# A hybrid decoder layer: the mixing's output product by Strassen's method, with low parts of its weight sums made by DMA

## The chip, the cores and the metric

One core of a Trainium2 chip runs the whole layer in one launch. The metric is device time in microseconds. TensorE multiplies, VectorE (DVE) and ScalarE (ACT) do elementwise work, GpSimd (POOL) does a little of it and issues DMAs of its own, SyncE (SP) issues the other DMAs.

## The reference, cut to what matters

A layer of 512 tokens, width 1024, with four sublayers, each followed by a LayerNorm of the weighted residual: a SwiGLU FFN, a token mixing, a cross-attention into 256 memory tokens, and another SwiGLU FFN. The mixing and what follows it:

```python
o = o * rsqrt(mean(o**2) + eps) * gnorm * silu(g)      # four gated heads, 512 channels
p = causal_multiscale_pool(v, pool_w, pool_scale)      # four pool groups, 512 channels
merged = concatenate([o, p], axis=-1)                  # (512, 1024)
h = layernorm(ALPHA * h + merged @ w_mix_out)          # w_mix_out (1024, 1024)
h = layernorm(ALPHA * h + memory_attention(h, mem, wq, wk, wv, wo))
```

The change concerns `merged @ w_mix_out`.

## The kernel before

**Numbers in two parts.** Every operand of a large product is held as a high and a low part in a reduced 32-bit format. `split` (L66 to L68) makes them: ScalarE casts the high part (L67), VectorE subtracts it from the source for the low one (L68). A product is then three matmuls: high by high, high by low, low by high (`mm3`, L55). `wblock` (L71) loads a weight block of 128 x 1024 by SyncE (L74) into one of 7 `raw` buffers and splits it, into two of 7 `q` buffers or, with `stay`, into one of the 13 large `b8` buffers. `one_behind` is called once for each weight block; it may send one action of a list (below) on GpSimd's queue, behind a tiny `seen` operation (L322) that waits for the block's high part.

**Order.** Each engine runs its own list of instructions in order. A planner makes these lists from the code: where an instruction's inputs or buffers aren't expected yet, a later one that is ready goes ahead. So transposes that the code puts ahead of a product stand in the trace between its matmuls.

**The two FFNs by Strassen's method.** `strassen_gemm` (L325) computes an FFN's output product from quarters of both sides with seven half-size products instead of eight, over three pairs of PSUM banks u, v and w: a11 by b11, s1 by t1, s2 by t2, a12 by b21, s4 by b22, s3 by t3, a22 by t4. The left sums are made by VectorE just ahead (`combine`, L347). The right sums t1 to t4 are sums of weight blocks: class `Sums` copies one block to a DRAM tile (`copy`, L281) and adds another by an accumulating DMA (`add`, L290), all on GpSimd's queue. The results go into h by L378 (with the residual's scale) and L381 (without).

**The mixing.** Projections by TensorE for the forget gates (`pf`), queries (`pq`), pool groups (`pv`), values (`vps`) and output gates (`pgt`), then the levels of the chunked scan, the states, and for each of four token tiles the output o: matmuls L876 and L878, squares on ScalarE, `rs` by a power on GpSimd (L886), the scaled o by VectorE (L887). The keys of the memory tokens are one `mem_key(k)` each (24 matmuls of 128 x 256): key 0 ahead of the states, 1 and 2 between the o tiles and their transposes (`ot`, L898), 3 to 7 after the output product. Each transposed tile is gated (L900) into `og` and split into `mg`; the pool groups have been split into `mg` by `pool_out`.

**Its output product.** `out_gemm` (called for "mo") goes over two halves of 512 columns. In a half it takes four weight blocks of 256 rows in the order 2, 3, 0, 1: the pool's first, then the heads'. The first blocks run block by block over four token tiles, the last ones (two in the first half, all four in the second) tile by tile, so that tile after tile is finished: L240 adds the bank to h, L243 takes statistics, `ln_tile` (L167 to L180, with a power on GpSimd, L174) normalises, `transpose_h` (L192) transposes into `moT` for the next stage. There is then `mem_key(3)` to `mem_key(7)`, and the memory's values `vm`, neither of which needs `moT`.

**The second FFN's sums.** From the queries on, two of three weight blocks send an action of the second FFN's list; what is left goes inside that FFN (`Sums.step`, L307).

Of the kernel before, what the change touches and what calls it, by code (L numbers as in the profile page):

```python
# [21 lines left out]
FF = 2816  # L22
FT = FF // P
H = 4
NMEM = 256
LEVELS = [1, 2, 4, 8, 16, 32, 64]
ALPHA = 2.0 ** 0.25
LN_EPS = 1e-5
# [6 lines left out]
def layer_kernel(ctx: ExitStack, tc: tile.TileContext, a, out):  # L35
    nc = tc.nc
# [4 lines left out]
    sm = ctx.enter_context(tc.tile_pool(name="sm", bufs=6))  # L41
    st = ctx.enter_context(tc.tile_pool(name="st", bufs=4))
# [20 lines left out]
    def raw4(shape, name):  # L63
        return wp.tile(shape, F32, tag="raw", name=name, bufs=7)

    def split(src, hi, lo, cast=nc.scalar.copy):  # L66
        cast(out=hi, in_=src)  # L67
        nc.vector.tensor_tensor(out=lo, in0=src, in1=hi.bitcast(F32), op=ALU.subtract)  # L68


    def wblock(src, name, stay=False):  # L71
        n = src.shape[-1]
        raw = raw4([P, n], f"raw_{name}")
        nc.sync.dma_start(raw, src)  # L74
        if stay:
            both = b8([P, 2, n], F32R, f"ws_{name}")
            hi, lo = both[:, 0, :], both[:, 1, :]
        else:
            hi, lo = q4([P, n], f"whi_{name}"), q4([P, n], f"wlo_{name}")
        split(raw, hi, lo)  # L80
        one_behind(hi)
        return hi, lo

# [182 lines left out]
    class Sums:  # L266
# [16 lines left out]
        def add(self, behind):  # L283

            if self.adds and self.adds[0] in self.T:
                p, b = self.adds.pop(0)
                x = {"t1": lambda: of_block(self.w, 1, self.kb1[b]), "t3": lambda: of_block(self.w, 1, self.kb2[b]),
                     "t2": lambda: self.T["t1", b], "t4": lambda: self.T["t2", b]}[p]()
                with tc.issue_after(behind):
                    nc.gpsimd.dma_start(self.T[p, b], x, accum_op=ALU.add, max_dma_last_dim=8192)  # L290
# [34 lines left out]
    def strassen_gemm(groups, S_, alpha, g, b, eps, name, final=False, pre=None, ys=None):  # L325
# [61 lines left out]
        if len(groups) == 1:  # L387
            quarter_["s1"] = [raw4([P, 4, 256], f"{name}s1")]
        else:
            s1 = b8([P, 2, 4, 256], F32, f"{name}s1")  # L390
            s1_ = [sm.tile([P, n, 256], F32, tag="s1", name=f"{name}s1_{n}", bufs=2) for n in (2, 1)]
            quarter_["s1"] = [s1[:, 0], s1[:, 1], *s1_]
        product(L, "b11", u, True)
        combine("s1", "a21", "a22", ALU.subtract)
        L = left("s1")
# [56 lines left out]
        if final or ys is not None:  # L452
            return None if final else tiles
        return [(tiles[k // 2][:, k % 2, 0, :], tiles[k // 2][:, k % 2, 1, :]) for k in range(KT)]


    def proj_T(w, X, n=S, name="pj"):
# [259 lines left out]
    def mslot(k):  # L717
        return mg[k // 2][:, k % 2, 0, :], mg[k // 2][:, k % 2, 1, :]

    pooled = {}  # L720

    def pool_in(g):
# [73 lines left out]
    for li, m in enumerate(LEVELS):  # L796
        tv = Tl[li].rearrange("p (n two) -> p n two", two=2)
        for g in range(2):
# [3 lines left out]
            if m < 64:  # L802
                def right(x, src=False):

                    return (x.rearrange("p (n two m) -> p n two m", two=2, m=m)[:, :, 1, :] if src
                            else x.rearrange("p (n m) -> p n m", m=m))
# [56 lines left out]
                    op0=ALU.mult, op1=ALU.add)  # L863
        states.append(Sn)

    for q in range(2):
        mg[q] = b8([P, 2, 2, S], F32R, f"mg{q}")


    os_ = []  # L870
# [22 lines left out]
    for c, o in enumerate(os_):  # L893
        cs = slice(c * P, (c + 1) * P)
        pt = tr_ps("ot")
        for hd in range(H):
            hs = slice(hd * P, (hd + 1) * P)
            nc.tensor.transpose(pt[:, hs], o[:, hs], ident)  # L898
        og = sm.tile([P, S], F32, tag="sg", name="og")
        nc.vector.scalar_tensor_tensor(  # L900
            out=og.rearrange("p (h d) -> p h d", h=H), in0=pt.rearrange("p (h d) -> p h d", h=H),
            scalar=gn[:, 0:1], in1=GS[:, :, cs], op0=ALU.mult, op1=ALU.mult)
        ov = og.rearrange("p (a b n) -> p a b n", a=2, b=2)
        for q in range(2):
# [174 lines left out]
```

## Time and profile before

| | us |
|---|---|
| median of 3 runs (lowest, highest) | 1041.16 (1040.78, 1041.31) |
| the profiled execution | 1040.28 |
| its span, first to last instruction | 1038.5 |
| TensorE busy | 1024.5 |
| VectorE busy | 830.7 |
| ScalarE busy | 508.3 |
| GpSimd busy | 137.4 |

The profile is of one execution. Its rows name line, engine, operation, output and inputs by the program's tile names, shapes and count, then busy time in us and the mean duration of one in ns, and after a second bar the idle time of the engine just ahead of them and what ended it. Matmuls overlap, so 390 ns for one is its latency; the spacing of consecutive ones is what counts. A stage row gives the window, its length, each engine's busy time with the number of instructions, the granted clock, the DMA engines' share and GB/s.

### The profile page before, as it was taken

What the parts mean: (1) busy time and instruction counts of PE and PEld (TensorE: products, weight loads), DVE (VectorE), ACT (ScalarE), POOL (GpSimd) and SP (SyncE); (2) the same over time, 40 slices, a digit from 0 to 9 for tenths busy, and PEclk for the clock granted to TensorE, in tenths of its full rate; (3) what the DMA queues carried; (4) which work ended last, traced back from release to release, by engine and by line L of the source; (5) the groups of instructions that cost most, each with busy time, mean ns of one, the idle gap of its engine ahead of it and who ended that gap; (6) DMA issues with size and microseconds to landing.
All of it is one profiled execution on the core that took longest, in us unless ns stands there. A gap on an engine that the chain in (4) does not pass through costs nothing. (4 is left out here: it accounts for less than half of the span.)

```text
span 1038.5 us, 17839 instructions
## 1 busy us (share of the span) xinstructions
PE 1024.5 (99%) x6898; PEld 926.9 (89%) x6898; DVE 830.7 (80%) x1360; ACT 508.3 (49%) x879; POOL 137.4 (13%) x212
## 2 busy tenths in 40 slices
PE   9999999999999999999999999999999999999995
PEld 8999999998887988879888988889999999988884
DVE  7999888889989645886686356589988888889885
ACT  5566555566644422235324345236555555565731
POOL 0011111215200101002212100110000000025000
PEclk9999999999999999999999999999999999999998
DMA  9375776578966455544819741603333332359761
GB/s 359 130 243 164 220 230 201 144 232 263 285 212 241 145 155 150 148 128 131 239 60 339 207 110 61 203 23 123 90 104 124 100 102 86 119 178 241 240 236 68
DMA packets 46148, 177.36 MB, mean 171 GB/s; under 512 B 6512, under 2 KB 7792, under 8 KB 42736
## 3 DMA queue, kind: packets, MB, share of 16 engines
q1 hardware_dynamic: 40176, 130.09, 36.3%
q0 software_dynamic: 5888, 46.14, 18.0%
q8 instruction: 54, 0.88, 0.3%
q14 instruction: 30, 0.25, 0.1%
HBM read 174.11 MB, written 48.23 MB: 214 GB/s over the span
## 5 line engine op out<-in xcount | busy, mean ns | idle before, releaser
L547 PE MATMUL f2u<-xt,qf2s 128*128 128x256 f32 x480 | 60.7, 283 | 0.0
L547 PE MATMUL f1u<-xt,qf1s 128*128 128x256 f32 x480 | 60.7, 283 | 0.0
L547 PEld LDWEIGHTS f1u<-xt,qf1s 128*128 128x128 f32 x480 | 59.0, 192 | 0.0
L547 PEld LDWEIGHTS f2u<-xt,qf2s 128*128 128x128 f32 x480 | 59.0, 192 | 0.0
L174 POOL TENSOR_TENSOR rstd<-ve,mhalf 128x1 f32<-128x1 f32 x16 | 15.6, 973 | 153.9 <-DVE ve L172 153.9
L68 DVE TENSOR_TENSOR wlo_wv<-raw_wv,whi_wv 128x1024 fp32r<-128x1024 f32 x12 | 14.7, 1224 | 23.4 <-PE pq L57 8.5
L547 PE MATMUL f2w<-xoT,qf2a 128*128 128x256 f32 x240 | 32.1, 284 | 0.0
L547 PE MATMUL f1u<-xT,qf1a 128*128 128x256 f32 x240 | 32.1, 283 | 0.0
L547 PE MATMUL f2u<-xoT,qf2a 128*128 128x256 f32 x240 | 32.1, 283 | 0.0
L547 PE MATMUL f1w<-xT,qf1a 128*128 128x256 f32 x240 | 32.1, 284 | 0.0
L307 POOL TENSOR_TENSOR seen<-qf2a,mhalf 128x1 f32<-128x1 f32 x10 | 5.9, 593 | 188.2 <-ACT qf2a L67 188.2
L547 PE MATMUL f1u<-xt,qf1a 128*128 128x256 f32 x240 | 30.7, 284 | 0.0
L547 PE MATMUL f1v<-xt,qf1s 128*128 128x256 f32 x240 | 30.7, 284 | 0.0
L547 PE MATMUL f2v<-xt,qf2s 128*128 128x256 f32 x240 | 30.4, 284 | 0.0
L547 PE MATMUL f1v<-xT,qf1s 128*128 128x256 f32 x240 | 30.4, 283 | 0.0
L547 PE MATMUL f2v<-xoT,qf2s 128*128 128x256 f32 x240 | 30.4, 284 | 0.0
L547 PE MATMUL f2u<-xt,qf2a 128*128 128x256 f32 x240 | 30.4, 283 | 0.0
L547 PEld LDWEIGHTS f1w<-xT,qf1a 128*128 128x128 f32 x240 | 30.3, 192 | 0.1
L547 PEld LDWEIGHTS f2w<-xoT,qf2a 128*128 128x128 f32 x240 | 30.3, 192 | 0.0
L547 PEld LDWEIGHTS f1u<-xT,qf1a 128*128 128x128 f32 x240 | 30.2, 192 | 0.0
L547 PEld LDWEIGHTS f2u<-xoT,qf2a 128*128 128x128 f32 x240 | 30.2, 192 | 0.0
L547 PEld LDWEIGHTS f1u<-xt,qf1a 128*128 128x128 f32 x240 | 29.6, 192 | 0.1
(435 smaller groups left out, 3305.8 us busy)
## 6 DMA issues: line engine op xcount, KB each, us to landing
f1t<-in_w1out POOLq DMA_DIRECT2D x30, 512.0 KB, 8.0
f2t<-in_w2out POOLq DMA_DIRECT2D x30, 512.0 KB, 6.6
raw_f1t<-f1t SPq DMA_DIRECT2D x20, 512.0 KB, 4.4
raw_f2t<-f2t SPq DMA_DIRECT2D x20, 512.0 KB, 4.9
raw_f2g<-in_w2in SPq DMA_DIRECT2D x17, 512.0 KB, 3.7
raw_f2u<-in_w2in SPq DMA_DIRECT2D x17, 512.0 KB, 3.8
raw_f1u<-in_w1in SPq DMA_DIRECT2D x15, 512.0 KB, 5.9
raw_f1b<-in_w1out SPq DMA_DIRECT2D x15, 512.0 KB, 7.5
```

The lines of the kernel that those rows point to most:

```text
L68: nc.vector.tensor_tensor(out=lo, in0=src, in1=hi.bitcast(F32), op=ALU.subtract)
L174: nc.gpsimd.tensor_tensor(out=rstd, in0=ve, in1=mhalf[:, 0:1], op=ALU.pow)
L307: ins = nc.gpsimd.tensor_tensor(out=seen, in0=q[:, 0, 0:1].bitcast(F32), in1=mhalf[:, 0:1], op=ALU.mult).ins
L547: nc.tensor.matmul(o, q[:, w, wsl], x[k][r], start=opens and k == 0 and n == 0, stop=ends and k == 3 and n == 2, skip_group_check=True)
```

## The change

- The product goes to a new function, `strassen_heads`: seven half-size products of 24 matmuls, left side A1 (pool groups) and A2 (heads) held unsplit in 32 bits (`mgp`, `mgh`) and cut into token halves. `pool_out` and the gating of heads write those and split nothing.
- b22, t3 and t4 run tile by tile (`by_tiles`); after b22 tiles 0 and 1 are normalised, after t4 tiles 2 and 3.
- For the right sums t1 to t4 (eight blocks) the low part comes in another way: ScalarE writes the high part, then its negative into the low part's place, and an accumulating DMA from GpSimd adds the source block to it in SBUF.
- All transposes of h stand behind keys 3 to 7 (`fill`).
- The product's own right sums (8 copies, 8 adds) are put ahead of the second FFN's list, which now starts at the forget gates with an action per weight block; no action during this product and the attention's output product, four of five blocks in between.
- In `strassen_gemm` a branch for a single group goes, which neither FFN took.

```diff
-    def wblock(src, name, stay=False):
+    def wblock(src, name, stay=False, by_dma=False):
...
-        split(raw, hi, lo)
+        if by_dma:
+            nc.scalar.copy(out=hi, in_=raw)
+            nc.scalar.activation(lo, hi.bitcast(F32), AF.Copy, scale=-1.0)
+            nc.gpsimd.dma_start(lo, src, accum_op=ALU.add, max_dma_last_dim=8192)
+        else:
+            split(raw, hi, lo)
         one_behind(hi)
...
+    def strassen_heads(A1, A2, S_, alpha, g, b, eps, name, ys=None, fill=None, pre=None):
...
+        A = {"a11": A1[:, :, lo], "a12": A2[:, :, lo], "a21": A1[:, :, hi], "a22": A2[:, :, hi]}
+        direct = {"b11": (0, S_.kb1), "b21": (0, S_.kb2), "b22": (1, S_.kb2)}
...
+        def left(p):
+            T = b8([P, 4, 2, 256], F32R, f"{name}{p}")
+            split(A[p], T[:, :, 0, :], T[:, :, 1, :])
+            return parts(T)
...
+        def right(p):
+            for i in range(2):
+                if p in direct:
+                    yield wblock(S_.w[direct[p][0], direct[p][1][i]], f"{name}{p}{i}")
+                else:
+                    yield wblock(S_.T[p, i], f"{name}{p}{i}", True, True)
...
+        A["s1"] = raw4([P, 4, 256], f"{name}s1")
+        product(left("a11"), "b11", u, True)
+        combine("s1", "a21", "a22", ALU.subtract)
+        L = left("s1")
+        for t in range(2):
+            add(t, 0, u[t], True)
+        product(L, "t1", v, True)
+        combine("a21", "a11", "a21", ALU.subtract)
+        combine("a11", "s1", "a11", ALU.subtract)
+        L = left("a11")
+        for t in range(2):
+            add(2 + t, 1, v[t], True)
+        product(L, "t2", u)
+        L = left("a12")
+        for t in range(2):
+            add(t, 1, u[t], True, ALU.subtract)
+        product(L, "b21", w, True, True)
+        combine("a12", "a12", "a11", ALU.add)
+        L, L3 = left("a12"), left("a21")
+        for t in range(2):
+            add(t, 0, w[t], False, last=True)
+        B22, T3 = list(right("b22")), list(right("t3"))
+        L4, T4 = left("a22"), list(right("t4"))
+        GB = ln_bcast(g, b)
+        for t in by_tiles(L, B22, v, True):
+            add(t, 1, v[t], False, last=True)
+            ln_tile(t, stats[t], GB, eps)
+        for t in by_tiles(L3, T3, u):
+            add(2 + t, 1, u[t], False, ALU.subtract, last=True)
...
+        for t in by_tiles(L4, T4, u, True):
...
+            add(2 + t, 0, u[t], True, last=True)
+            ln_tile(2 + t, stats[2 + t], GB, eps)
...
+        if fill is not None:
+            fill()
+        for t in range(0 if fill is not None else 2, NT):
+            transpose_h(t, tiles, ys)
...
+    sums_mo = Sums(a["wmixo"], "mo", [2, 3], [0, 1])
+    sums2 = Sums(a["w2out"], "f2", *FFN_BLOCKS)
+    todo_behind += sums_mo.actions() + sums2.actions()
+    pace[:] = 0, 1, 1
     pf01 = proj_T2(wf, X1, "pf")
...
-    sums2 = Sums(a["w2out"], "f2", *FFN_BLOCKS)
-    todo_behind += sums2.actions()
-    pace[:] = 0, 2, 3
...
-    mg = {q: b8([P, 2, 2, S], F32R, f"mg{q}") for q in (2, 3)}
...
+    mg = [None, b8([P, 4, S], F32, "mgp")]
...
-        mh, ml = mslot(4 + g)
-        nc.scalar.activation(mh, pm, AF.Copy, scale=psc[:, g:g + 1])
-        nc.vector.scalar_tensor_tensor(out=ml, in0=pm, scalar=psc[:, g:g + 1], in1=mh.bitcast(F32),
-                                       op0=ALU.mult, op1=ALU.subtract)
+        nc.scalar.activation(mg[1][:, g, :], pm, AF.Copy, scale=psc[:, g:g + 1])
...
-        og = sm.tile([P, S], F32, tag="sg", name="og")
         nc.vector.scalar_tensor_tensor(
-            out=og.rearrange("p (h d) -> p h d", h=H), in0=pt.rearrange("p (h d) -> p h d", h=H),
+            out=mg[0][:, :, cs], in0=pt.rearrange("p (h d) -> p h d", h=H),
...
-        for q in range(2):
-            split(ov[:, q], mg[q][:, :, 0, cs], mg[q][:, :, 1, cs])
-
-    X2 = out_gemm(a["wmixo"], KT, mslot, ALPHA, a["ln2_g"], a["ln2_b"], LN_EPS, "mo", order=[2, 3, 0, 1])
...
-    for k in range(3, KT):
-        mem_key(k)
+    def more_keys():
+        pace[:] = 0, 4, 5
+        for k in range(3, KT):
+            mem_key(k)
+
+    pace[:] = 0, 0, 1
+    X2 = strassen_heads(mg[1], mg[0], sums_mo, ALPHA, a["ln2_g"], a["ln2_b"], LN_EPS, "mo", fill=more_keys)
...
     ys, wx = [], []
+    pace[:] = 0, 0, 1
     X3 = out_gemm(a["wo"], KT, lambda k: (OT[k // 2][:, k % 2, 0, :], OT[k // 2][:, k % 2, 1, :]),
```

More of the change, by code (lines that the diff above doesn't have):

```diff
@@ L386, in strassen_gemm @@
         L = left("a11")
[L387 to L392, printed above, removed]
+        s1 = b8([P, 2, 4, 256], F32, f"{name}s1")
+        s1_ = [sm.tile([P, n, 256], F32, tag="s1", name=f"{name}s1_{n}", bufs=2) for n in (2, 1)]
+        quarter_["s1"] = [s1[:, 0], s1[:, 1], *s1_]
         product(L, "b11", u, True)
@@ L454, in strassen_gemm, with combine, block, product @@
         return [(tiles[k // 2][:, k % 2, 0, :], tiles[k // 2][:, k % 2, 1, :]) for k in range(KT)]
+    def strassen_heads(A1, A2, S_, alpha, g, b, eps, name, ys=None, fill=None, pre=None):
+        stats = [st.tile([P, 2, 6], F32, tag=f"stats{t}", name=f"stats{t}", bufs=1) for t in range(NT)]
+        lo, hi = slice(0, 256), slice(256, 512)
+        A = {"a11": A1[:, :, lo], "a12": A2[:, :, lo], "a21": A1[:, :, hi], "a22": A2[:, :, hi]}
[4 more added lines that the diff above has]
+            return parts(T)
+        def combine(o, x, y, op):
+            nc.vector.tensor_tensor(out=A[o], in0=A[x], in1=A[y], op=op)
+        def right(p):
[3 more added lines that the diff above has]
+                else:
+                    assert (p, i) in S_.T and (p, i) not in S_.adds
+                    yield wblock(S_.T[p, i], f"{name}{p}{i}", True, True)
+        def block(t, i, w, L, ps, opens, ends):
+            tsl = slice(t * P, (t + 1) * P)
+            for j in range(2):
+                k, csl = 2 * i + j, slice(j * 512, (j + 1) * 512)
+                ah, al = L[k][0][:, tsl], L[k][1][:, tsl]
+                for n, (x, y) in enumerate(((ah, w[0]), (ah, w[1]), (al, w[0]))):
+                    nc.tensor.matmul(ps, x, y[:, csl], start=opens and k == 0 and n == 0, stop=ends and k == 3 and n == 2,
+                                     skip_group_check=True)
+        def product(L, p, ps, opens=False, ends=False):
+            for i, w in enumerate(right(p)):
+                for t in range(2):
+                    block(t, i, w, L, ps[t], opens, ends)
+        def by_tiles(L, ws, ps, ends=False):
+            for t in range(2):
+                for i, w in enumerate(ws):
+                    block(t, i, w, L, ps[t], False, ends)
+                yield t
+        def add(t, hf, ps, scale, op=ALU.add, last=False):
+            sl = slice(hf * 512, hf * 512 + 512)
+            if scale:
+                nc.vector.scalar_tensor_tensor(out=h[t][:, sl], in0=h[t][:, sl], scalar=float(alpha), in1=ps,
+                                               op0=ALU.mult, op1=op)
+            else:
+                nc.vector.tensor_tensor(out=h[t][:, sl], in0=h[t][:, sl], in1=ps, op=op)
+            if last:
+                nc.vector.bn_stats(stats[t][:, hf, :], h[t][:, sl])
+        u, v, w = ([mm_ps(f"{name}{n}{t}") for t in range(2)] for n in "uvw")
+        A["s1"] = raw4([P, 4, 256], f"{name}s1")
[12 more added lines that the diff above has]
+        L = left("a12")
+        for t in range(2):
+            add(t, 1, u[t], True, ALU.subtract)
+        product(L, "b21", w, True, True)
+        combine("a12", "a12", "a11", ALU.add)
+        L, L3 = left("a12"), left("a21")
+        for t in range(2):
+            add(t, 0, w[t], False, last=True)
[7 more added lines that the diff above has]
+            add(2 + t, 1, u[t], False, ALU.subtract, last=True)
+        tiles = [quarter(f"{name}T{q}") if ys is not None else b8([P, 2, 2, S], F32R, f"{name}T{q}") for q in range(4)]
+        if fill is None:
+            transpose_h(0, tiles, ys)
+        for t in by_tiles(L4, T4, u, True):
+            if fill is None and t == 0:
+                transpose_h(1, tiles, ys)
+            add(2 + t, 0, u[t], True, last=True)
+            ln_tile(2 + t, stats[2 + t], GB, eps)
+            if t == 0 and pre is not None:
+                pre()
+        if fill is not None:
+            fill()
+        for t in range(0 if fill is not None else 2, NT):
+            transpose_h(t, tiles, ys)
+        return (tiles if ys is not None else
+                [(tiles[k // 2][:, k % 2, 0, :], tiles[k // 2][:, k % 2, 1, :]) for k in range(KT)])
@@ L864, in layer_kernel @@
         states.append(Sn)
-    for q in range(2):
-        mg[q] = b8([P, 2, 2, S], F32R, f"mg{q}")
+    mg[0] = b8([P, 4, S], F32, "mgh")
     os_ = []
```

4 lines of the change are left out of this document (removed).

## Prediction

> **What bounds the kernel now.** I read the page first, then who waits for whom on TensorE, then the busy times by stage.
>
> ```profile
> span 1038.5 us, 17839 instructions
> PE 1024.5 (99%) x6898; PEld 926.9 (89%) x6898; DVE 830.7 (80%) x1360; ACT 508.3 (49%) x879; POOL 137.4 (13%) x212
> PEclk9999999999999999999999999999999999999998
> ```
> ```profile
> PE idle L103 <- DVE mhalf L157: 1.1, 1, 1.1
> PE trh L192 <- DVE h L180: 0.5, 1, 0.5
> PE po L56 <- ACT PT L67: 0.2, 1, 0.2
> PE f2u L367 <- DVE h L381: 0.2, 1, 0.2
> ```
> ```profile
> 230.00:260.00 30.00, 30.00 (x133) 24.79 (x132) 29.92 (x34) 19.20 (x24) 16.48 (x14) 1.00 0.79 254
> 260.00:300.00 40.00, 40.00 (x178) 33.08 (x177) 36.23 (x42) 22.03 (x27) 6.82 (x13) 1.00 0.90 275
> 490.00:505.00 15.00, 15.00 (x74) 12.33 (x73) 12.57 (x19) 7.46 (x14) 3.95 (x8) 1.00 0.94 252
> 505.00:523.00 18.00, 18.00 (x81) 14.67 (x80) 11.71 (x18) 3.16 (x3) 3.60 (x5) 1.00 0.67 226
> 523.00:538.00 15.00, 14.97 (x78) 11.99 (x78) 12.31 (x26) 3.15 (x9) 1.54 (x2) 1.00 0.01 4
> 538.00:554.00 16.00, 16.00 (x133) 15.65 (x132) 14.04 (x25) 8.54 (x16) 4.20 (x7) 1.00 0.69 224
> 493.30:522.90 29.60, 29.60 (x130) 24.28 (x130) 3.43 (x5) 1.00 0.81 239
> ```
>
> The page says TensorE 99% at full clock. The four waits are all that this view lists for TensorE in the whole span: 2.0 us. In the stage table the columns are length, then busy time of TensorE, weight loads, VectorE, ScalarE and GpSimd, granted clock, DMA share, GB/s. The mixing's output product (490 to 538) runs with TensorE busy throughout and VectorE at 65 to 84%. The last row counts that product's own matmuls in its densest stretch: 130 in 29.60 us, 0.2277 us each, one after the other. So the end is set by the list of TensorE's work: a matmul taken out is worth 0.2277 us, unless a new wait takes its place.
>
> The Trainium skill, page "Perfetto Trace Analysis", section Identifying the Most-Contended Engine, warns that matmul busy time overstates how close TensorE is to its limit and points to the weight loads instead. Here they are busy 24.28 of 29.60 us, 82%; by that rule a fifth of the stretch could be slack, and 24 matmuls fewer would bring about 4.5 us. I go by the even spacing and the missing waits.
>
> **What is removed.**
>
> ```profile
> L223 PE MATMUL mops<-whi_mo,mg 128*128 128x512 f32 x40 | 16.0, 399 | 0.0
> L223 PE MATMUL mops<-ws_mo,mg 128*128 128x512 f32 x24 | 9.4, 394 | 0.0
> L68 DVE TENSOR_TENSOR wlo_mo<-raw_mo,whi_mo 128x1024 fp32r<-128x1024 f32 x5 | 6.1, 1220 | 2.6 <-PE pk L58 1.5 <-issue 1.1
> L67 ACT CAST whi_mo<-raw_mo 128x1024 fp32r<-128x1024 f32 x5 | 5.2, 1047 | 0.0
> L240 DVE SCALAR_TENSOR_TENSOR h<-h,mops 128x512 f32<-128x512 f32 x8 | 5.5, 685 | 7.4 <-PE mops L225 7.3
> L243 DVE BATCH_NORM_STATS2 stats<-h 128x6 f32<-128x512 f32 x8 | 5.5, 693 | 0.2
> L177 DVE SCALAR_TENSOR_TENSOR h<-h,mv,G 128x512 f32<-128x512 f32 x8 | 5.6, 744 | 0.0
> L180 DVE SCALAR_TENSOR_TENSOR h<-h,rstd,B 128x512 f32<-128x512 f32 x8 | 5.6, 747 | 0.1
> L68 DVE TENSOR_TENSOR mg<-og,mg 128x256 fp32r<-128x256 f32 x8 | 2.9, 419 | 0.0
> L900 DVE SCALAR_TENSOR_TENSOR og<-ot,gn,GS 128x512 f32<-128x512 f32 x4 | 2.9, 745 | 0.0
> L68 DVE TENSOR_TENSOR wlo_wk<-raw_wk,whi_wk 128x1024 fp32r<-128x1024 f32 x6 | 7.3, 1212 | 0.4 <-PE pgt L57 0.3
> L68 DVE TENSOR_TENSOR KM<-pk,KM 128x256 fp32r<-128x256 f32 x6 | 2.5, 422 | 0.4 <-ACT KM L67 0.2
> ```
>
> L223, L224 and L225 issue one matmul each, so there are 3 x (40 + 24) = 192. Seven half-size products of 2 weight blocks x 2 token tiles x 2 x 3 are 168. Gone: 24 x 0.2277 = 5.46 us of TensorE's list. The transposes stay 32 and keys 3 to 7 stay 5; they only change place. One Strassen product is 24 x 0.2277 = 5.46 us, and all that feeds it must keep that pace.
>
> **What is added on VectorE.** Sums of quarters are tensor_tensor on 128x1024, as in the FFN products; adds into h without the scale too:
>
> ```profile
> L347 DVE TENSOR_TENSOR f1g<-f1g,f1g x2: 1218/1218/1219, 266.7 to 268.5; 128x1024 f32<-128x1024 f32 x2
> L381 DVE TENSOR_TENSOR h<-h,f1w x2: 670/674/679, 290.2 to 292.5; 128x512 f32<-128x512 f32 x2
> 484.10 0.39 PE L878 MATMUL o<-Sall,QP 128*128 128x128 f32 x2
> 487.78 0.69 DVE L887 TENSOR_TENSOR o<-o,rs 128x512 f32<-128x512 f32 x1 [1.12 <-POOL rs L886]
> 489.58 1.04 PE L898 MATMUL ot<-ident,o 128*128 128x128 f32 x8
> 538.50:546.20 7.70, 7.70 (x64) 7.56 (x63) 0.85 (x2) 0.74 (x2) 1.00 0.39 113
> ```
>
> The last row is of the keys' matmuls alone: 7.70/64 = 0.12 us each, 2.89 us for a key of 24.
>
> First the chain to the second product. Before, two pool blocks (48 matmuls, 10.9 us) stood ahead of anything that needs the heads; now only the a11 product (5.46 us) does. The last head tile is normalised at 488.5. Then VectorE has two key halves (0.84), four gated heads (2.98), the s1 sum (1.22), ScalarE's cast (1.05), s1's low part (1.22): 7.3 us, ready at 495.8. The eight splits L68 of heads (2.9) are gone from there. TensorE has 16 transposes (2 x 1.04) and one product from 489.58: it wants s1 at 497.1. The slack is 1.3 us, one weight split of 1.22 slipped in uses it up, two make TensorE wait 1.1 us. I take 0.4 (bounds 0 and 1.1).
>
> Then the pace. From 488.5 to the end of the fourth product (497.1 + 3 x 5.46 = 513.5) VectorE gets: heads and keys 3.82, four sums 4.88, five left low parts 6.10, four right ones 4.88 (b21, b22), six adds 4.11: 23.8 us in 25.0, 95%. With the low parts of t1 and t2 on VectorE too it would be 28.7, over the room; the DMA takes these. The first FFN's Strassen stretch, the two rows from 230 to 300, had VectorE at 29.92 of 30 and 36.23 of 40 and TensorE lost nothing. I take 0.2 for it (bounds 0 and 1).
>
> A new wait: t4's first tile goes into the bank that t3 filled, after VectorE has added that bank to h. Only t3's second tile (2.73 us) stands between, and VectorE then has the LayerNorms of tiles 0 and 1 queued. No transposes stand between as they do in the first FFN. The nearest row is f2u waiting 0.2 for L381. The upper end is a LayerNorm's last four operations ahead of that 0.67 add: 2.98 + 0.67 - 2.73 = 0.9. I take 0.3, near the row.
>
> **What is added on ScalarE, GpSimd and DMA.** Eight right blocks get a second ScalarE pass (8 x 1.05 us; ScalarE is busy 7.46 of 15.00 at most) and an accumulating DMA from GpSimd into SBUF. No such transfer into SBUF is in the trace; accumulating ones in DRAM are:
>
> ```profile
> f2t<-f2t POOLq DMA_DIRECT2D x10, 512.0 KB, 7.3
> L290 POOL DMA_DIRECT2D f2t<-f2t x12: 763/796/854, 420.9 to 956.7; - x12
> DMA to landing us min/median/max: 4.3/7.1/9.5
> ```
>
> Of the 13 large buffers 11 or 12 hold QP, scT, V, GS, Sall, the merged halves, memory, keys and a11 until the last o matmul ends at 484.5. From there, the second t1 block needs up to four ScalarE passes (4.2), the issue (0.80) and the landing (7.3): 496.8, and 499.0 with the worst landing. TensorE wants it half a product after 497.1, at 499.8. t2, t3 and t4 are wanted 5 us or more later each, with buffers free earlier than that. So I cost it at nothing; the cover is the a11 product and keys 1 and 2 ahead of it. If the landing took twice the median, as could be with DMA at 0.94, t1 would be 4.3 us late.
>
> The Trainium skill, page "DMA: Bandwidth & Descriptors", section Anatomy of one DMA (SWDGE path), fits 2.0 us plus bytes over 436e3 per us: an estimate of 3.2 us for 512 KB. The trace's 7.3 us is more than twice that. By the page t1 would land at 492.7 and the late-landing rival below would vanish; the sum stays.
>
> GpSimd's queue is in order: a transfer that waits for ScalarE's second pass holds what stands behind it, the rs and rstd powers. rs stands on the head chain, so a t1 issue placed ahead of it costs it up to 0.80 us each; it is within the 0.4 above. SyncE loads 14 blocks instead of 16 for this product.
>
> Moved: 16 actions for this product's sums go ahead of the second FFN's on GpSimd, one per weight block from the forget gates on, and the last goes out behind the second gate's block, with two gates, three keys and the o stage still ahead of the product. More of the second FFN's sums then run inside that FFN. The first FFN runs all its sums inside itself, with no TensorE wait in the list above. Nothing is charged (bounds 0 and 0.5). Keys 3 to 7, with loads and splits, stand behind t4 instead of behind the transposes; the transposes then run beside 96 matmuls of the values (21.9 us) that don't need them, so the LayerNorm tail is hidden.
>
> **Sum.** -5.46 + 0.4 + 0.2 + 0.3 = -4.56. The profiled execution took 1040.28 (span 1038.5), the median of the runs is 1041.16, 0.88 above it; I take the difference off the median: 1036.6.
>
> **Rivals.** *Low parts late.* TensorE waits for SBUF-accumulating DMAs at t1 and, less, at t2. For: 512 KB into SBUF was never timed, DMA 0.94 at 490 to 505. Against: GpSimd and ScalarE have room and the later three have time. Price 2 to 5 us above the sum: 1039 to 1041, about no change.
>
> *VectorE's tail starves the keys* (slower). The first FFN's tail shows the small steps of a LayerNorm, and what else stands there:
>
> ```profile
> 306.26 0.20 DVE L170 BATCH_NORM_AGGREGATE mv<-stats 128x2 f32<-128x12 f32 x1
> 306.37 1.18 DVE L68 TENSOR_TENSOR wlo_f1t<-raw_f1t,whi_f1t 128x1024 fp32r<-128x1024 f32 x1
> 307.45 0.15 DVE L172 TENSOR_SCALAR ve<-mv 128x1 f32<-128x1 f32 x1
> ```
>
> From the end of the fourth product VectorE has: two w tiles 2 x (0.67 + 0.69) = 2.73, a22's low part 1.22, two v tiles, two t3 tiles 2.73, two t4 tiles. A tile with LayerNorm is 0.69 + 0.69 + 2 x 0.74 + 2 x 0.75 + 0.35 = 4.71, so 25.5 in all, against three products of 16.4. When TensorE comes to key 3 VectorE is 9.1 us behind. If a key's low part (1.21) stood behind all that, TensorE would wait 10.3 us: 1041.16 - 5.46 + 0.6 + 10.3 = 1046.6. Each key split ahead of the backlog covers 2.89 us; it decides below two: with one, 1043.7, with two 1040.8. Against it are the three rows: in the first FFN's tail a weight split is placed inside a LayerNorm, between two of its dependent steps, so later weights don't stand behind it.
>
> *The saving isn't there.* If the gain follows the weight loads it is 4.5 instead of 5.46: 1037.6, inside the range.
>
> **Chances.** Forecast (with the smaller saving) 0.78; late low parts 0.14, a third of it still faster; starved keys 0.08, three quarters of it slower. 0.2% is 2.1 us, about what a measurement tells from no change. Faster (under 1039.1): 0.78 + 0.05 = 0.83. Slower: 0.06. Same: 0.11. The range: its low end is the full 5.46 and half a microsecond more from the waits that TensorE has now, 1035.2. The bounds above add 1.1 + 1 + 0.9 + 0.5 - 0.9 taken = 2.6 to the sum, 1039.2; up to 1039.6 it takes in the near part of the late landings and leaves out under 2 in 10.
>
> **What would show it.** Right: TensorE's matmul count 24 lower, busy near 1020, its wait list under 4 us, accumulating transfers into SBUF landing in 5 to 9 us. Wrong: a wait of TensorE on a DMA (the first rival), on the keys' or values' low parts by L68 (the second), on s1's left part by more than 1.1 us, or on h at t4 by more than 0.9; or TensorE without such waits and a gain under 4 us, which would say that matmuls were not worth their spacing.

## The result and the profile after

The changed kernel takes 1054.87 us (median), where the kernel before took 1041.16. Single runs far above the others of their kernel, one of 2043.85 us here, count in the medians and are left out of the ratios and intervals; without it the runs here go from 1051.94 to 1055.54, with a median of 1054.31. The ratio is 1.0124, with a 95% interval of 1.0108 to 1.0141: 12.9 us more (11.2 to 14.7), where 4.6 us less was forecast. The profiled execution took 1055.54.

First the changed kernel's page: span, busy times, TensorE's granted clock in 40 slices.

```profile
span 1053.7 us, 17870 instructions
PE 1022.8 (97%) x6874; PEld 924.4 (88%) x6874; DVE 836.9 (79%) x1363; ACT 526.5 (50%) x892; POOL 160.8 (15%) x238
PEclk9999999999999999999899999999999999999997
```

6898 - 6874 = 24 matmuls are gone, as forecast, but TensorE now waits for something that it never waited for before. Its waits (us in total, times, longest):

```profile
PE mov L489 <- DMA ws_mot<-mot: 8.7, 2, 6.7
PE mou L489 <- DMA ws_mot<-mot: 3.6, 3, 1.9
PE idle L109 <- DVE mhalf L163: 1.1, 1, 1.1
PE pk L56 <- ACT whi_wk L67: 1.0, 1, 1.0
PE ot L995 <- DVE mgh L996: 0.8, 1, 0.8
PE mou L489 <- DVE moa L68: 0.6, 1, 0.6
```

`ws_mot` are the blocks of t1 to t4, `mov` the second product (by t1), `mou` those by t2, t3 and t4. The first two rows are the accumulating transfers into SBUF. TensorE's own timeline at t1 (start, length, instruction; in brackets the idle time ahead of it):

```profile
498.72 0.61 PE L489 MATMUL mov<-ws_mot,mos 128*128 128x512 f32 x2
506.06 4.48 PE L489 MATMUL mov<-ws_mot,mos 128*128 128x512 f32 x11 [6.72 <-DMA ws_mot<-mot]
512.50 4.11 PE L489 MATMUL mov<-ws_mot,mos 128*128 128x512 f32 x10 [1.95 <-DMA ws_mot<-mot]
```

Two matmuls with the high part run, then the low part is missing for 6.72 us, and half a product later the second block's is missing for 1.95. There is more: 11 matmuls at 0.2277 us are 2.5 us, and here they take 4.48. The stage table (columns as before) has the reason: the granted clock is 0.66 and 0.83 there.

```profile
490.00:500.00 10.00, 7.94 (x41) 5.92 (x38) 9.55 (x12) 5.13 (x6) 0.64 (x1) 1.00 0.23 69
500.00:510.00 10.00, 3.94 (x10) 3.16 (x11) 4.33 (x4) 9.22 (x10) 2.88 (x4) 0.66 0.98 258
510.00:520.00 10.00, 7.87 (x27) 5.66 (x25) 3.78 (x5) 1.39 (x3) 0.00 (x0) 0.83 0.98 256
```

Why so late? The rows of these blocks (minimum, median and maximum in ns, first and last start in us), the time from issue to landing of all eight transfers, and then that of t1's two alone:

```profile
L82 ACT CAST ws_mot<-raw_mot x8: 1028/1040/1052, 496.9 to 527.5; 128x1024 fp32r<-128x1024 f32 x8
L84 POOL DMA_DIRECT2D ws_mot<-mot x8: 857/865/936, 499.4 to 530.7; - x8
DMA to landing us min/median/max: 6.7/10.5/13.6
```
```profile
ws_mot<-mot POOLq DMA_DIRECT2D x1, 512.0 KB, 6.7
ws_mot<-mot POOLq DMA_DIRECT2D x1, 512.0 KB, 9.4
```

ScalarE starts on t1 at 496.9, though its large buffers are free from 484.5, when the last o matmul ends (here too it starts at 484.1). ScalarE's timeline shows what stands ahead:

```profile
490.09 1.05 ACT L67 CAST moa<-mgp 128x1024 fp32r<-128x1024 f32 x1
495.96 1.05 ACT L67 CAST mos<-mos 128x1024 fp32r<-128x1024 f32 x1 [4.82 <-DVE mos L473]
496.92 1.04 ACT L82 CAST ws_mot<-raw_mot 128x1024 fp32r<-128x1024 f32 x1
500.78 1.04 ACT L67 CAST moa<-mgp 128x1024 fp32r<-128x1024 f32 x1 [0.79 <-DVE mgp L473]
501.73 1.05 ACT L83 ACTIVATE ws_mot<-ws_mot 128x1024 fp32r<-128x1024 f32 x1
```

ScalarE idles 4.82 us in front of the cast of s1, which waits for the heads, and t1's first cast stands behind it on the list. So t1 begins when s1 is ready, and TensorE can't multiply by its low part until two ScalarE passes, an issue (at 499.4) and a landing of 6.7 us later, at 506.06. The second block's second pass stands behind the cast of the next left part, the last two rows; it is issued at 503.1 and lands 9.4 us later, at 512.5.

Last, one row each of before and of after that I had not looked at: GpSimd's last instruction, a drain, from its last power on. The maximum is the one that counts.

```profile
L1075 POOLq DRAIN  x3: 40/93/8944, 1028.8 to 1038.2; - x3
```
```profile
L1173 POOLq DRAIN  x3: 46/102/10909, 1042.0 to 1053.5; - x3
```

It sets the end of both spans (1028.8 + 8.9 = 1037.7, then 0.8 us of closing semaphores) and is 1.96 us longer after. The rest lies in the mixing's output product and the keys, as the first matmuls of the next stage, the cross-attention's queries, say for before and after:

```profile
L56 PE MATMUL pxq<-moT,whi_wxq x80: 277/389/397, 575.8 to 628.7; 128*128 128x512 f32 x48, 128*128 128x256 f32 x32
```
```profile
L56 PE MATMUL pxq<-moT,whi_wxq x80: 277/389/396, 590.3 to 643.2; 128*128 128x512 f32 x48, 128*128 128x256 f32 x32
```

They start at 575.8 and 590.3, the first transposes of heads at 489.6 in both. Between these, the starts of TensorE's matmuls give: 24 matmuls fewer, -5.46; gaps of over 0.3 us beyond the spacing, +16.9 (before had none); the slow matmuls and smaller gaps, +3.0: together +14.5. The rest of the span gives back 1.25, nearly all of it in the second FFN, and the drain adds 1.96: 15.2, which is 1053.7 - 1038.5.

### The profile page after: what moved, and what is told of

The parts are those of the page before. It is cut to its first block, busy times and chain, and to the rows that moved or that the text cites. A ratio compares the mean times of both kernels' runs of the same rounds, so it can differ in the third digit from the quotient of the medians.

```text
span 1053.7 us, 17870 instructions
## 1 busy us (share of the span) xinstructions
PE 1022.8 (97%) x6874; PEld 924.4 (88%) x6874; DVE 836.9 (79%) x1363; ACT 526.5 (50%) x892; POOL 160.8 (15%) x238
## 5 line engine op out<-in xcount | busy, mean ns | idle before, releaser
L313 POOL TENSOR_TENSOR seen<-qf1a,mhalf 128x1 f32<-128x1 f32 x10 | 5.5, 555 | 179.2 <-ACT qf1a L67 136.9
L68 DVE TENSOR_TENSOR wlo_wv<-raw_wv,whi_wv 128x1024 fp32r<-128x1024 f32 x12 | 14.7, 1223 | 19.1 <-PE pq L57 8.4
```

Source lines behind the costliest of these rows:

```text
L313: ins = nc.gpsimd.tensor_tensor(out=seen, in0=q[:, 0, 0:1].bitcast(F32), in1=mhalf[:, 0:1], op=ALU.mult).ins
```

## The experiments

Theory A: the low parts are late, first because t1 to t4 are begun too late on the in-order lists, then because a transfer into SBUF lands late. Theory B: VectorE and ScalarE can't feed seven products of 5.46 us, and whatever is mended, a wait on them takes its place. The drain came up later. (The Theory C in one expectation is another one: that the tail is late because keys stand ahead of the transposes.) Each result gives the time, its ratio to the kernel before and the 95% interval of the ratio; versions of different groups of runs are set beside each other by these ratios, as the kernel before, run in each group, took from 1040.31 to 1041.16 us.

**All low parts by VectorE.**

```diff
-                    yield wblock(S_.T[p, i], f"{name}{p}{i}", True, True)
+                    yield wblock(S_.T[p, i], f"{name}{p}{i}", True)
```

> The changed kernel with the low parts of t1 to t4 made by VectorE's subtraction again, nothing else undone. Theory A (the accumulating DMAs land late: 12.3 us of TensorE's waits and some 3 us of slow matmuls behind them): these go, little comes in their place, 1037 to 1040 us. Theory B (VectorE can't keep the products' pace, with or without the DMA; 28.7 us of its work for 25.0): the wait moves to VectorE's low parts, 1042 to 1047 us.

1050.81 us, ratio 1.0102 (1.0086 to 1.0117), above both lines. The waits on DMA are gone and others stand there:

```profile
PE mou L489 <- DVE h L509: 3.8, 2, 2.8
PE mov L489 <- DVE ws_mot L68: 1.5, 1, 1.5
PE mou L489 <- DVE ws_mot L68: 1.5, 1, 1.5
PE pk L56 <- ACT whi_wk L67: 1.4, 1, 1.4
```

So B holds when VectorE does all of it (busy 10.00 of 10 from 520 to 540). The first row is the wait for h at t4 that I had put at 0.3.

**t1 begun early.**

```diff
+    t1 = [wblock(sums_mo.T["t1", i], f"mot1{i}", True, True) for i in range(2)]
...
     mg[0] = b8([P, 4, S], F32, "mgh")
```

> The changed kernel with t1's two blocks taken, cast and sent to the accumulating DMA ahead of the buffer for the merged heads, some 20 us earlier; t2 to t4 unchanged. Theory A, in the form that t1's chain starts late because large buffers are granted in the order of the code: TensorE's wait on t1 (8.7 us) and the slow matmuls behind it (3.4 us) go, the 3.6 us at t3 and t4 stay: 1042 to 1044 us. If instead an accumulating transfer into SBUF is slow whenever it is sent (over 15 us): a wait of 5 us or more stays at t1, 1048 us and more.

1048.58 us, 1.0086 (1.0067 to 1.0105). The wait at t1 is gone (its casts now start at 475.5), so A is right on t1, though the time is above its 1042 to 1044. The next transfer is late instead, and two places that lost their order pay:

```profile
PE mou L489 <- DMA ws_mot<-mot: 4.5, 1, 4.5
PE mow L489 <- ACT whi_mob L67: 2.8, 1, 2.8
PE ot L998 <- DVE mgh L999: 2.3, 1, 2.3
```

The last row is GpSimd's in-order queue: its second t1 issue, at 481.74, waited for ScalarE, and the four `rs` powers behind it ran from 483.2 instead of 481.0.

**TensorE kept busy at t1.** Thirty dummy matmuls of 128x512 into a bank not yet in use, between the first product and t1's (`warm_l` is a11's left part); the result is the same.

```diff
+        for i in range(30):
+            nc.tensor.matmul(w[0], warm_l[:, 0, 0, :P], warm_l[:, 0, :, :], start=True, stop=True, skip_group_check=True)
```

> The changed kernel with 30 matmuls of 128x512 more (6.8 us, their result is overwritten) between the first product and t1's, where TensorE waits 7 us. If the doubled spacing (0.43 us) of the matmuls behind the wait comes from the clock that was granted after TensorE's idleness: the wait's end stays where it is, the spacing is 0.23 again, and the time falls by 3 to 4 us to about 1051. If it comes from something else at that time (DMA load, late buffers): spacing stays 0.43, no change, 1054 to 1055 us.

1054.33 us, 1.0139 (1.0122 to 1.0155): no gain, where 3 to 4 us were expected if it is the clock. Yet the clock is whole again:

```profile
500.00:510.00 10.00, 9.21 (x41) 7.24 (x39) 4.42 (x5) 9.21 (x11) 3.48 (x4) 1.00 0.94 244
510.00:520.00 10.00, 6.42 (x26) 4.35 (x24) 5.21 (x6) 3.97 (x6) 0.00 (x0) 1.00 1.04 278
```

So the slow matmuls follow from the idle time. They cost next to nothing here, as TensorE, back at full speed, waits for the next landing at 512.8 instead of 512.5.

**Keys behind the transposes again.**

```diff
-    X2 = strassen_heads(mg[1], mg[0], sums_mo, ALPHA, a["ln2_g"], a["ln2_b"], LN_EPS, "mo", fill=more_keys)
+    X2 = strassen_heads(mg[1], mg[0], sums_mo, ALPHA, a["ln2_g"], a["ln2_b"], LN_EPS, "mo")
+    more_keys()
```

> The changed kernel with keys 3 to 7 behind the transposes, as the other Strassen products have it: transposes of tiles 0 and 1 between t3 and t4. Theory A has no part in this: within 1 us of the changed kernel. Theory C (the tail is late because keys stand ahead of the transposes; TensorE's waits of 1.0 for a key's high part and 0.8 for transposes): 1 to 2 us faster, or as much slower if the transposes wait for VectorE's LayerNorms.

1061.59 us, 1.0206 (1.0188 to 1.0223), far above both lines. That part of the change gains 7 us or more:

```profile
PE mov L489 <- DMA ws_mot<-mot: 8.4, 1, 8.4
PE trh L198 <- DVE moT L68: 4.1, 1, 4.1
```

**No accumulating transfer into SBUF.** The low parts of t1 to t4 stay the negative of the high ones, so this part of the product isn't computed.

```diff
-            nc.gpsimd.dma_start(lo, src, accum_op=ALU.add, max_dma_last_dim=8192)
```

> The changed kernel without the eight accumulating DMAs into SBUF: the low parts of t1 to t4 stay the negative of the high ones, so the product is another one; ScalarE's two passes stay. Theory A: the waits on the DMA (12.3 us) and the slow matmuls go and what is left of waits is 3 to 5 us: 1038 to 1041 us. Rival: under these waits lie others of nearly the same length (ScalarE's passes, VectorE's chain), as when VectorE made the low parts: 1044 to 1050 us.

1042.55 us, 1.0018 (1.0009 to 1.0028), between the two lines. By the ratios, late transfers and what hangs on them are thus some 11 of the 12.9 us; 0.65 of that is the last drain, 10.26 us long here. Even without them 5.46 us of matmuls fewer bring nothing; its longest waits in this stage:

```profile
PE pk L56 <- ACT whi_wk L67: 1.4, 1, 1.4
PE pk L58 <- DVE wlo_wk L68: 0.8, 1, 0.8
PE ot L994 <- DVE mgh L995: 0.8, 1, 0.8
PE mov L488 <- ACT ws_mot L83: 0.7, 1, 0.7
PE mou L488 <- DVE moa L68: 0.6, 1, 0.6
```

**Loads held back.** The loads of b22, t3 and t4 were to wait until t1's product is in h (`behind`), so as not to share the DMA engines with t1's transfers.

```diff
...
+            with tc.issue_after(behind):
+                nc.sync.dma_start(raw, src)
```

> The changed kernel with the loads of b22, t3 and t4 held back until t1's product has been added to h, so that fewer loads run beside the accumulating DMAs of t1 and t2. If these land late because they share the DMA engines with the loads: they land in 5 to 7.5 us instead of 6.7 to 11.8, TensorE's waits on t1 and t2 fall by 3 to 5 us: 1049 to 1052 us. If the transfer itself takes that long: landing 9 us and more, 1054 to 1056 us.

1054.94 us, 1.0136 (1.012 to 1.0152); landing 6.3/10.2/13.1. The edit held nothing back. SyncE's loads of t3 and t4, in the changed kernel and then in this one:

```profile
501.20 9.04 SPq L74 DMA_DIRECT2D raw_mot<-mot  x4
501.33 9.04 SPq L78 DMA_DIRECT2D raw_mot<-mot  x4
```

The VectorE operation that they were to wait for runs at 516.2, after all of them. So this is the changed kernel once more, and whether the loads beside them make the transfers land late stays open.

**A plain transfer.** The low parts are then the whole sums, so the product is another one.

```diff
-            nc.gpsimd.dma_start(lo, src, accum_op=ALU.add, max_dma_last_dim=8192)
+            nc.gpsimd.dma_start(lo, src, max_dma_last_dim=8192)
```

> The changed kernel with the four right sums' transfers plain instead of accumulating: the low parts are then the whole sums, so the product is another one. If accumulating into SBUF is what makes a transfer of 512 KB land after 10.5 us, the landing falls to 4 to 6 us and TensorE's wait at t1 from 8.7 to 3 or 4 us: 1047 to 1050 us. If the landing comes from what else the DMA engines do then, it stays near 10 us and the time near 1055 us.

1047.8 us, 1.0071 (1.0056 to 1.0086), and

```profile
DMA to landing us min/median/max: 4.7/6.6/7.3
```

Accumulating into SBUF takes 10.5 instead of 6.6 us for 512 KB, and by the ratios that is 5.5 of the 12.9 us. Here too t1's casts start late (497.6), and TensorE waits 4.9 us at t1.

**t1 by VectorE and a11's left part ahead of `mgh`, t2 by DMA ahead of s1.**

```diff
+    ws = {"t1": [wblock(sums_mo.T["t1", i], f"mot1{i}", True, False) for i in range(2)]}
...
+    a11 = b8([P, 4, 2, 256], F32R, "moa11")
+    split(mg[1][:, :, :256], a11[:, :, 0, :], a11[:, :, 1, :])
     mg[0] = b8([P, 4, S], F32, "mgh")
...
+        ws["t2"] = [wblock(S_.T["t2", i], f"{name}t2{i}", True, True) for i in range(2)]
-        product(left("a11"), "b11", u, True)
+        product(a11, "b11", u, True)
```

> The changed kernel with three things moved up in the code: t1's blocks (low parts by VectorE's subtraction) and a11's left parts stand ahead of the buffer for the merged heads, t2's blocks (by DMA as in the change) ahead of the first product; t3 and t4 unchanged. Theory A (what costs is that the right blocks of t1 and t2 come late, since large buffers are granted in the order of the code): no wait of TensorE on t1, t2 or their DMAs, 1 to 3 us of others: 1037 to 1041 us. Theory B (VectorE's chain from the heads through s1 is too slow for 5.46 us of product whatever the right side does): waits of 3 us or more on s1's or the next left parts, 1042 to 1046 us.

1045.27 us, 1.0047 (1.0034 to 1.006): the time is in B's range, but there is no wait at t1 and t2 any more and none on s1 or the next left parts. What is left on DMA is t3 and t4:

```profile
PE mou L489 <- DMA ws_mot<-mot: 4.3, 2, 3.4
```

**The same with t2 by VectorE.**

```diff
-        ws["t2"] = [wblock(S_.T["t2", i], f"{name}t2{i}", True, True) for i in range(2)]
+        ws["t2"] = [wblock(S_.T["t2", i], f"{name}t2{i}", True, False) for i in range(2)]
```

> As e5_t1_t2_ahead, with t2's low parts by VectorE too, so that only t3 and t4 use the accumulating DMA. 2 x 1.22 us of VectorE more, between 485 and 505: theory A (time is there once the buffers are): within 1 us of e5_t1_t2_ahead. Theory B: each of the 2.4 us comes out as a wait: 2 us and more above e5_t1_t2_ahead.

1046.77 us, 1.006 (1.0046 to 1.0074): the same wait on t3 and t4, and 0.7 for s1's cast. It is 1.5 us above the run beside it, between the two lines; the intervals overlap, so it isn't shown that the transfer serves t2 better.

**t3 ahead of the t2 product, t4 ahead of the b21 product.** On top of the version with t1 and t2 ahead:

```diff
+        T3 = list(right("t3"))
         product(L, "t2", u)
...
+        T4 = list(right("t4"))
         product(L, "b21", w, True, True)
```

> As the kernel with t1 by VectorE and t2 ahead of s1 (1045.3 us), but with the blocks of t3 begun ahead of the t2 product and those of t4 ahead of the b21 product, all four still by accumulating transfer. If the late start of t3 and t4 is what is left, TensorE's wait for their transfers (4.3 us there) goes, with the slow spacing of 0.43 behind it (some 20 matmuls, about 3 us): 1038 to 1041 us. If the pace of VectorE and ScalarE is what is left, the casts that now stand earlier hold up a12 and its sums by 1 to 2 us each, and the time stays at 1043 to 1046 us.

1041.25 us, 1.0008 (0.9999 to 1.0017). No wait on a transfer is left in TensorE's list:

```profile
PE mow L489 <- ACT whi_mob L67: 2.1, 1, 2.1
PE idle L109 <- DVE mhalf L163: 1.1, 1, 1.1
PE ot L1003 <- DVE mgh L1004: 0.8, 1, 0.8
PE mow L489 <- DVE wlo_mob L68: 0.5, 1, 0.5
```

So the order, together with t1's low parts on VectorE and all else as the change has it, takes back 12.1 of the 12.9 us and makes the kernel as fast as before. What order alone gives isn't shown: no run has all four sums early and t1 by transfer. The 5.5 us of the plain transfers are no further part beside these 12.1: both shorten the same waits.

**One step later each.**

```diff
+        T3 = list(right("t3"))
         product(L, "b21", w, True, True)
...
+        T4 = list(right("t4"))
         L, L3 = left("a12"), left("a21")
```

> The same with t3 begun ahead of the b21 product and t4 between the b21 product's sums and a12's second left part: each one step later than in the run beside it. The late start theory: t3 is issued some 5 us earlier than in the kernel with t1 and t2 ahead and its wait goes, t4 has 2 us of its own left at most: 1040 to 1043 us. The pace theory: less is pushed ahead of the left parts, so it is no slower than the run beside it.

1047.91 us, 1.0073 (1.0061 to 1.0086): no wait on a transfer either, but 3.8 us for a key's low part and 3.1 for VectorE's LayerNorm steps. The pace theory's line for this run was a miss as well: less pushed ahead, and slower.

**b21 ahead of t3.** In the version of 1041.25 the first row is a cast of b21 behind those of t3 and t4.

```diff
+        ws["b21"] = list(right("b21"))
         T3 = list(right("t3"))
```

> The kernel with all four sums begun early (1041.3 us), with the two blocks of b21 fetched and split ahead of t3's ScalarE passes. There TensorE waits 2.1 us for a ScalarE cast of b21 that stands behind the passes of t3 and t4, and 0.5 for its low part. If order on ScalarE's list is what is left, these 2.6 to 3.0 us go: 1038.0 to 1038.7 us. If VectorE's pace is what is left, the waits come back at a12's left parts or at the keys: 1040.5 to 1041.5 us.

1044.42 us, 1.0037 (1.0025 to 1.0049), above both lines. That wait is gone, and TensorE, sooner at the keys, waits in key 4 (98 of the keys' matmuls are done):

```profile
PE pk L58 <- DVE wlo_wk L68: 3.6, 1, 3.6
PE mou L489 <- DMA ws_mot<-mot: 1.5, 1, 1.5
```

**Keys 3 and 4 split ahead of the t3 product.**

```diff
+        keys()
         for t in by_tiles(L3, T3, u):
...
+    def keys():
...
+        KW.update({k: wblock(a["wk"][k], f"wk{k}") for k in (3, 4)})
```

Here the two early blocks send an action of the second FFN's list each, and two of three blocks of the keys behind, instead of four of five.

The expectation has the key wrong: the wait of 3.6 us was in key 4.

> The kernel with all sums begun early and b21 ahead (1044.4 us), with the weights of keys 3 and 4 split ahead of the t3 product. There TensorE waits 3.6 us in key 3 for a low part that stands behind LayerNorm steps on VectorE. If that place on VectorE's list is what is left, the wait goes and nothing behind it is late, as the LayerNorms split by the keys feed transposes with 22 us of other matmuls beside them: 1039.5 to 1041.0 us. If it is VectorE's whole load, the wait comes back at a later key or at the transposes: 1043 to 1045 us.

1045.42 us, 1.0049 (1.0036 to 1.0062); the same row, now of 3.8, in key 5 (123 done). Keys 3 and 4 run without a wait, and the wait moved on to the next key, as B has it: VectorE is busy 10.00 of 10 from 530 to 540.

**The drain.** To the kernel before, 24 small transfers (256 bytes, read by nothing) are added on GpSimd's queue:

```diff
+    few = scr.tile([24, 64], F32, name="few")
+    for i in range(24):
+        nc.gpsimd.dma_start(few[i:i + 1], a["wmix"][FF_][i:i + 1, :64])
```

> The kernel before, with 24 small transfers of 256 bytes added on GpSimd's queue at the forget gates; nothing reads them. GpSimd's last drain lasts 8.94 us in the kernel before (96 transfers of its own), 10.25 with 112, 10.75 with 118, 10.91 with 120: 0.082 us for each. If the drain counts transfers, it lasts 10.9 us here, TensorE ends as before and the time is 1.9 to 2.0 us longer: 1042.4 us. If it goes by bytes or packets, or by what else the change does, the drain stays at 8.9 to 9.1 us and the time at 1040.4 us.

1042.2 us, 1.0018 (1.001 to 1.0027), so 1.7 more (1.0 to 2.8 by the interval), and the drain is that of the changed kernel to the nanosecond:

```profile
L1078 POOLq DRAIN  x3: 46/93/10909, 1028.1 to 1039.5; - x3
```

It counts transfers, not bytes. Then **fewer of them, in the kernel before**: the plain copies from SyncE.

```diff
-                with tc.issue_after(behind):
-                    nc.gpsimd.dma_start(T, x)
+                nc.sync.dma_start(T, x)
```

> The kernel before with the 48 plain copies of its two weight sums issued from SyncE's queue, which leaves GpSimd 48 transfers. By 0.082 us for each the last drain lasts 5.0 us instead of 8.94; the last output tile lands 4.6 us after the drain begins, so the end comes 3.9 us earlier: 1036.5 us. If the copies hold up the weights behind them, 1039 to 1048 us. Set beside the run before it, this says what the change is worth when both pay the same for GpSimd's transfers: some 2.5 to 3 us.

1037.12 us, 0.9967 (0.9955 to 0.9979), the fastest of all:

```profile
L1074 POOLq DRAIN  x3: 40/93/5036, 1029.4 to 1035.0; - x3
```

**The same edit in the version with b21 ahead**, then in the one with the keys' edit, for two of the three weight sums (`if self.name == "f1"` keeps the old lines) and for all:

> The kernel with all sums begun early and b21 ahead, with the 56 plain copies of all three weight sums (24, 8 and 24) issued from SyncE's queue instead of GpSimd's, which leaves GpSimd 62 transfers. By 0.082 us for each, the last drain lasts 6.2 us instead of 10.75 and the end comes 4.6 us earlier: 1033.5 to 1034.5 us. If the copies on SyncE's queue hold up the weights behind them, TensorE waits for raw weights in the two FFNs and the gates and the gain is lost: 1036 to 1045 us.

> The kernel with the keys split early, with the 32 plain copies of the mixing's and the second FFN's sums issued from SyncE's queue; those of the first FFN stay on GpSimd, as with all on SyncE that FFN took 4.7 us more in the profiled run. GpSimd keeps 86 transfers: a last drain of 8.1 us instead of 10.75, so 2.6 us less than the run beside it: 1037 to 1038.4 us if that is at 1040. If SyncE's copies hold up other weights in the gates or the second FFN, no gain or a loss of some us.

> The same with all 56 plain copies on SyncE's queue, 62 transfers left on GpSimd: a drain of 6.2 us, 4.6 us less than the run with the keys split early: 1035 to 1036.5 us if the first FFN is not disturbed (in the kernel before it was not). If it loses its 4.7 us again, the gain and the loss cancel: 1040 us.

1042.72 us (1.0021, 1.0011 to 1.0032), 1053.44 (1.0125, 1.011 to 1.014) and 1044.54 (1.0044, 1.003 to 1.0058). The drains are 6.18, 8.13 and 6.18 us, as worked out, but the first and the third gain only 1.7 and 0.9 us on the versions without the edit, and the second loses 8. In the first the first FFN takes nearly 5 us more; where the third loses its gain isn't shown. In the second the reason is plain:

```profile
L290 SPq DMA_DIRECT2D mot<-in_wmixo x8: 495/587/1047, 28.3 to 43.0; - x8
```
```profile
PE f1v L659 <- DVE qf1s L68: 7.4, 1, 7.4
```

Without a `seen` to wait for, SyncE's copies for the mixing go out at 28 us and those of the second FFN from 44 to 120, ahead of the first FFN's own weights. VectorE waits 11.26 us for one of these at 141.7, and TensorE behind it at 143.0. No version of the change beat the kernel before with its copies on SyncE.

## Why the prediction was wrong

**The step that failed** is the one on the low parts, "So I cost it at nothing". It let t1's ScalarE passes begin at 484.5, when buffers come free. They began at 496.9: on ScalarE's list they stand behind s1's cast, which I had myself put at the end of the chain of heads, ready at 495.8. So the cover that I named, the a11 product and two keys, had passed. The landing wasn't what failed at t1: its two transfers took 6.7 and 9.4 us, where I took 7.3 from accumulations in DRAM with 9.5 as the worst. Begun some 12 us late, they cost TensorE 8.7 us; begun at 475.5 in the run with t1 early, none. Behind t1 the landing was off too: t2, t3 and t4, which I said had time, landed after up to 13.6 us and cost 3.6 us. These 12.3 us of waits, and what hangs on them, are some 11 us of time by the run without transfers. The rival *low parts late* named the place and the kind of wait rightly, and was priced at 2 to 5 us by the same early start.

The rule of the Trainium skill (DMA: Bandwidth & Descriptors, Anatomy of one DMA, SWDGE path) gave an estimate of 3.2 us; the runs disagree with it for 512 KB here, beside other loads, even without accumulating (6.6 us, 4.7 at least).

The rival *The saving isn't there* wasn't borne out: this product's matmuls stay 0.227 us apart where nothing holds them up, so each one taken out was worth that, not 82% of it.

**Right.** 24 matmuls fewer; and the tail with the keys ahead of the transposes is worth the 7 us or more that its undoing costs. The second FFN's sums cost nothing (that FFN became 1.2 us shorter).

**Too small.** The chain to s1, put at 0.4 with bounds 0 and 1.1. A low part of b11 (at 488.4) and a11's (at 492.8) stand between the heads on VectorE's list, the two splits that were to cost 1.1, and s1 was ready at 498.3 instead of 495.8. TensorE waited ahead of it, 0.8 us for gated heads (`ot`) and 0.6 for a11's low part, and came to s1 at 498.7 without a further wait.

The pace of VectorE and the wait at t4, 0.2 and 0.3. With the transfers left out, four of the five rows shown (without `ot`) still hold 3.5 us of waits on VectorE and ScalarE, and in the version with all sums early there are 2.6 beside `ot`. The wait at t4 shows in neither; it is 3.8 where VectorE makes all low parts. The sum counted busy time, 95% of the room, and took the first FFN for proof that this fits. The rows show single casts and splits that are late at the head of an in-order list, which a sum of busy times doesn't hold.

**The rival *VectorE's tail starves the keys*** was right as a mechanism. With two keys split ahead of the backlog it was to be 1043.7 - 1040.8 = 2.9 us cheaper than with one; the versions with a faster front show 3.6 with one (key 4 waits) and 3.8 with two (key 5 waits), so a key ahead doesn't buy what I said. The changed kernel itself, where TensorE comes to the keys some 15 us later, has no wait on a key's low part, only 1.0 on a high one.

**Missing altogether.** The last drain: 24 GpSimd transfers more, 1.96 us. I had read waits on TensorE only, and the row stood in the profile of before. With this term (22 transfers in that version) and the waits that are left with all sums early, 3.4 with `ot`, the forecast becomes -5.46 + 3.4 + 1.8 = -0.3: no change, which is what that version measured (1.0008).

## What to carry to other kernels

Price an operation from the place where it stands on its engine's in-order list, not from when its inputs and buffers are there: an idle engine may be waiting at the head of the list. Before trading instructions of the bounding engine for work elsewhere, write the start and the end of each new chain (passes, issue, landing) against the moment when it is wanted. Look at what ends the span after the last useful instruction; a cost per transfer can hide there.

## What the runs showed of the hardware

GpSimd's last drain grows by 0.082 us with each transfer that GpSimd has issued, whatever its size: 5.04 us with 48, 8.94 with 96, 10.25 with 112, 10.75 with 118, 10.91 with 120 (the same whether 24 of these are of 256 bytes or of 512 KB). The Trainium skill (VectorE: DVE Perf Modes, The DRAIN you can't avoid) puts the drains that the runtime adds at a kernel's two ends at about 12 ns on all engines. This one bears a line of the kernel, so it may be of another kind; no run here settles that.

An accumulating transfer of 512 KB into SBUF landed after 10.5 us (6.7 to 13.6), a plain one in the same place after 6.6 (4.7 to 7.3).

After 6.7 us of idleness TensorE ran at a spacing of 0.43 us instead of 0.23 for 3.5 us, and after 1.95 us, close behind that, again. The Trainium skill (TensorE: Matmul & The Clock Gate, What's actually happening) puts the clock at half after an idle window of about 3.4 us; the first agrees. The second idle time is shorter, and in the run with dummy matmuls a wait of 2.48 us left the clock whole; no run shows why it fell again.
